# Out projection of a hybrid decoder block: the conv half of a row tile ahead of the other half, the row chain cut into stages, weights loaded as whole rows

## The chip, the cores and the metric

One core of one Trainium2 chip. The metric is the time of one execution on the device in microseconds; the kernel before took 1990.24 us, the median of three runs from 1987.65 to 1991.64.

## The reference

A decoder block on `x` of shape (1, 2048, 1024), all in float32:

```python
hn = rms_norm(x, g_pre_mix)
proj = hn @ w_in                       # 1024 -> 512 (ssm) + 3 x 512 (conv)
y_ssm  = s5_group_mixer(u_ssm, ...)    # state-space scan, gelu, y * sigmoid(y @ w_glu)
y_conv = short_conv_mixer(h, b, c, conv_w)
y = concat([rms_norm(y_ssm, g_ssm_out), rms_norm(y_conv, g_conv_out)])
x = x + rms_norm(y @ w_out, g_post_mix)
hn = rms_norm(x, g_pre_mlp)
m = square(relu(hn @ w_up)) @ w_down
x = x + rms_norm(m, g_post_mlp)
```

`w_out` is 1024 x 1024: its rows 0 to 511 take the ssm half of `y`, rows 512 to 1023 the conv half.

## The kernel before

Every float32 product is made of three matmuls (`mm3`, L88 to L90): each operand is split into a high part (an ACT copy, L169) and a low part (a subtraction on DVE or POOL, L170). A product of 128 x 512 x 128 thus costs three TensorE instructions.

The sequence is written out in four parts. First the ssm input projection; then the conv projections (three per column tile and block of 512 positions, eight passes `n` of two blocks), with the state-space work hooked between them; then the **out projection**, which the change touches; then the MLP, whose two products are computed in seven partial products each (`ORDER`, `DORDER`). The orders of TensorE and of POOL (GpSimd) are as written; DVE (VectorE), ACT (ScalarE) and SP (the DMA queue) get their order from the planner, which places work by its estimate of readiness, with the program's order as priority, and runs it in order on the chip.

The out projection goes over four blocks of 512 positions, each of four row tiles `t` of 128 rows:

- `yprep(blk)` loads the state-space output of a block and splits it.
- `cprep(blk)` loads the conv output `yc_d` of a block (four tiles of 128 x 512), multiplies by `gcv`, splits into `b8` tiles, squares and sums (`sumsq`).
- `glu(blk)` multiplies by `w_glu` (48 matmuls into PSUM tag B), then sigmoid, product, gain `gss`, split, and on POOL squares (L794) and sums (L798).
- `norms(blk, br)` sums the squares over partitions by four small matmuls (L858, PSUM tag C) and takes the -1/2 power on POOL (L868). The result `rr` scales the rows of branch `br` (1 conv, 0 ssm).
- `branch(blk, t, br, ...)` multiplies a row tile by its half of `w_out` in two column halves `dh` of twelve matmuls each. Both branches take PSUM tag A (4 banks). The conv half leaves by ACT (L890), the ssm half is added by DVE (L892). `norms` is called after the first twelve matmuls of tile 0 in each branch.
- `rows_out(blk, t, o, xx)` is the row chain: sum of squares on ACT (L897), times gain (L898), `rstd` on POOL (L122, L123), residual (L900), write `x1_d`, sum of squares (L903), gain (L904), `rstd`, scale (L906), write `hn_d`.
- `load_wo` splits `w_out` in 16 steps of 128 x 512, each staged through an `s2k` tile; 8 steps for the conv half run inside `glu(0)`, 8 for the ssm half beside the conv branches of block 0.

Between the products, `next(aside)` takes one step of side work: `yprep` and `cprep` of the next block; in block 2 also `hsums`, which writes sums of quarters of the normed rows to `hs_d` (L946, L947); in block 3 `first()`, which prepares the MLP's first operands (`wprep`, `xbuild` with transposes L984). Buffers: `s2k` 9 tiles of 2 KB per partition, `b8` 14 and `c8` 4 tiles of 8 KB, `r4("o")` and `r4("xx")` 2 tiles of 4 KB each. In blocks 1 to 3 a row tile is done as

```python
branch(blk, t, 1, o, aside)
branch(blk, t, 0, o, aside)
rows_out(blk, t, o, xx)
```

while block 0 does all four conv branches first (into `os_`, two `c8` tiles).

Of the kernel before, what the change touches and what calls it, by code (L numbers as in the profile page):

```python
# [52 lines left out]
def block_kernel(  # L53
# [641 lines left out]
    def yprep(blk):  # L695
# [7 lines left out]
        for q in range(4):  # L703
# [34 lines left out]
    for n in range(8):  # L738
        hf, i = divmod(n, 4)
        for b in range(2):  # L740
            blk = 2 * hf + b
            if g == 45:
                pl.close()
                open_left()
                run(yprep(0))
                gluh, glul = c8(), c8()
                for k in range(4):
                    split2(gluh[:, k, :], glul[:, k, :], w_glu[k * P:(k + 1) * P, :], V)
            r2 = act.tile([P, BLK], F32, name="r2", bufs=2)
# [20 lines left out]
            V.tensor_tensor(yt, ps, c, op=ALU.mult)  # L770
# [15 lines left out]
    gcv = small("gcv", 4, 1)  # L786
    nc.sync.dma_start(out=gcv, in_=g_conv)


    def sumsq(blk, br, i, t):  # L790
        if br:
            A.activation(t, t, AF.Square)
        else:
            G.tensor_tensor(t, t, t, op=ALU.mult)  # L794
        if i == 0:
            sqs[blk, br] = t
        else:
            (V if br else G).tensor_tensor(sqs[blk, br], sqs[blk, br], t, op=ALU.add)  # L798

    def cprep(blk):  # L800
        h, l = b8(), b8()
        mc[blk] = (h, l)
        raw = {}
        for i in range(-2, 4):
            if i < 2:
                raw[i + 2] = s2k()
                nc.sync.dma_start(out=raw[i + 2], in_=yc_d[i + 2][:, blk * BLK:(blk + 1) * BLK])
                if i < 0:
                    continue
            if i == 0:  # L810
                yield
            yc = raw[i]
            A.activation(h[:, i, :], yc, AF.Copy, scale=gcv[:, i:i + 1])
            V.scalar_tensor_tensor(l[:, i, :], yc, gcv[:, i:i + 1], h[:, i, :].bitcast(F32),
                                   op0=ALU.mult, op1=ALU.subtract)
            sumsq(blk, 1, i, yc)
            yield

    def glu(blk):
        h, l = b8(), b8()  # L820
        mh[blk] = (h, l)
        for m in range(4):
# [5 lines left out]
            A.activation(sg, ps, AF.Sigmoid)  # L828
# [3 lines left out]
            A.activation(h[:, m, :], sg, AF.Copy, scale=gss[:, m:m + 1])  # L832
            V.scalar_tensor_tensor(l[:, m, :], sg, gss[:, m:m + 1], h[:, m, :].bitcast(F32),
                                   op0=ALU.mult, op1=ALU.subtract)
            sumsq(blk, 0, m, sg)
            if blk == 0:
                next(wo_steps)
                next(wo_steps)

    wo = {}  # L840

    def load_wo():
        for h in (1, 0):
            for k in range(4 * h, 4 * h + 4):
                wo[k] = b8()
            for dh in range(2):
                for k in range(4 * h, 4 * h + 4):
                    t = wo[k]
                    split2(t[:, 2 * dh, :], t[:, 2 * dh + 1, :],
                           w_out[k * P:(k + 1) * P, dh * 512:dh * 512 + 512], G if k % 2 else V)  # L850
# [22 lines left out]
    def junk():  # L873
        return sb["R"].tile([P, D], BF16, name="junk", bufs=1)

    def branch(blk, t, br, o, aside):

        m = (mc if br else mh)[blk]
        for dh in range(2):
            sl = slice(dh * 512, dh * 512 + 512)  # L880
# [7 lines left out]
            rr = rrs[blk, br]  # L888
            if br:
                A.activation(o[:, sl], ps, AF.Copy, scale=rr[:, t:t + 1])  # L890
            else:
                V.scalar_tensor_tensor(o[:, sl], ps, rr[:, t:t + 1], o[:, sl], op0=ALU.mult, op1=ALU.add)  # L892
            next(aside, None)

    def rows_out(blk, t, o, xx):
        s1 = small("s1", 4)
        A.activation(junk(), o, AF.Square, accum_out=s1[:, 0:1])  # L897
        V.tensor_tensor(o, o, gpo, op=ALU.mult)  # L898
        rstd(s1[:, 1:2], s1[:, 0:1], 1, 1.0 / D, s1[:, 2:3])
# [4 lines left out]
        V.tensor_tensor(o, xx, gmb, op=ALU.mult)  # L904
        rstd(s3[:, 1:2], s3[:, 0:1], 1, 1.0 / D, s3[:, 2:3])
# [4 lines left out]
    def wout(blk, aside, between=iter(())):  # L910
        def row_in(t):
            xx = r4("xx")
            tt = 4 * blk + t
            nc.sync.dma_start(out=xx, in_=x[tt * P:(tt + 1) * P, :])
            return xx

        if blk == 0:
            os_ = [z.rearrange("p (a b) c -> p a (b c)", b=2)[:, i, :] for z in (c8(F32), c8(F32)) for i in range(2)]
            for t in range(4):
                branch(blk, t, 1, os_[t], between)  # L920
            run(between)
        for t in range(4):
            xx = row_in(t)
            o = os_[t] if blk == 0 else r4("o")
            if blk:
                branch(blk, t, 1, o, aside)
            branch(blk, t, 0, o, aside)
            if t == 3:
                run(aside)
            rows_out(blk, t, o, xx)  # L930

# [54 lines left out]
            V.tensor_tensor(l[:, k, :], pt, h[:, k, :].bitcast(F32), op=ALU.subtract)  # L986
            yield

    cprep0 = cprep(0)
    next(cprep0)  # L990
    gss = sb["XR"].tile([P, 24], F32, name="gss", bufs=1)[:, :4]
    nc.sync.dma_start(out=gss, in_=g_ssm)
    run(cprep0)
# [27 lines left out]
    def first():  # L1021
# [334 lines left out]
```

## Time and profile before

| | |
|---|---|
| median of three runs | 1990.24 us (1987.65 to 1991.64) |
| the profiled execution | 1990.73 us, span 1988.8 us, mean granted clock 0.983 |
| TensorE busy (matmul) | 1920.9 us, 97% |
| VectorE, ScalarE, GpSimd busy | 71%, 44%, 37% |
| instructions | 25438 |

The span runs from the first to the last instruction of the profiled execution. Busy time is the share of the span in which an engine executes; on TensorE matmuls overlap, so a busy engine can still run slowly. Rows in order of time give start, duration, engine, line, operation and `out<-in` by the program's names, and in brackets how long the engine was idle before it and what released it. Rows of waits give who waited for whom, the total in us, the times and the longest. Rows of stretches give the length, then busy time and count of PE, PEld, DVE, ACT and POOL, the granted clock, the DMA share and GB/s.

### The profile page before, as it was taken

The page shows a single profiled execution, that of the slowest core. Times are in us where ns is not written, and L with a number is a line of the kernel's source. Part 1 is how long each engine was busy: PE and PEld are TensorE (multiplying, and loading weights), DVE is VectorE, ACT ScalarE, POOL GpSimd, SP SyncE. Part 2 cuts the span into 40 slices and gives each one's busy share as a digit, 9 for nine tenths or more (in the row PEclk, how much of TensorE's full clock was granted, in tenths as well). Part 3 has the DMA queues.
Part 4 walks back from the last instruction along what each step waited for, and adds up shares of the span by engine and source line. Part 5 has one row for each costly group of instructions (what it writes and reads, how often), then busy time and mean ns, then how long its engine had stood idle before and what let it go on. Part 6 is the DMA issues. An engine that isn't in the chain of part 4 may idle for free.

```text
span 1988.8 us, 25438 instructions
## 1 busy us (share of the span) xinstructions
PE 1920.9 (97%) x8576; PEld 1572.0 (79%) x8576; DVE 1402.3 (71%) x2007; ACT 865.4 (44%) x1479; POOL 741.4 (37%) x727
## 2 busy tenths in 40 slices
PE   8899999998899799999999999999999999999996
PEld 6677777776787678888888888887888888888885
DVE  8958889856666668998888878877644344539554
ACT  6322232226454355555566555554334242335321
POOL 3666556304534533434433434433522002104222
PEclk9899999998999899999999999999999999999998
DMA  6432343235546566555446434428955545538633
GB/s 203 133 101 75 99 123 115 70 90 160 179 157 194 189 243 218 211 204 204 170 166 238 158 143 148 148 86 312 382 168 180 187 147 180 195 107 301 236 114 111
DMA packets 202002, 340.34 MB, mean 171 GB/s; under 512 B 56336, under 2 KB 64784, under 8 KB 199568
## 3 DMA queue, kind: packets, MB, share of 16 engines
q1 hardware_dynamic: 200576, 336.62, 50.2%
q10 hardware_dynamic: 1296, 2.10, 0.3%
q8 instruction: 67, 1.10, 0.2%
q14 instruction: 63, 0.52, 0.1%
HBM read 230.51 MB, written 106.95 MB: 170 GB/s over the span
## 4 chain that ended last, share of the span: by engine, by line
PE 80%; POOL 6%; DMA 4%; DVE 4%; issue 3%; ACT 2%; SPq 0%; DVEq 0%; POOLq 0%; ACTq 0%
PE A L89 16%; PE A L88 16%; PE A L90 16%; PE mm L88 4%; PE mm L89 4%; PE mm L90 4%; PE B L88 4%; PE B L89 4%; PE B L90 4%; PE C L89 1%; PE C L88 1%; PE C L90 1%; DMA raw<-in_xt_dram 1%; PE B L984 1%; POOL s2k L794 1%
## 5 line engine op out<-in xcount | busy, mean ns | idle before, releaser
L1016 POOL TENSOR_TENSOR t<-b 128x512 f32<-128x512 f32 x155 | 243.8, 1595 | 358.6 <-ACT w2a L169 98.3
L1130 POOL TENSOR_TENSOR t<-t,t 128x512 f32<-128x512 f32 x80 | 116.8, 1468 | 356.1 <-DMA t<-in_w_down_dram 306.5
L88 PE MATMUL mm<-xh,wh 128*128 128x512 f32 x496 | 199.3, 402 | 7.8 <-ACT wh L169 7.3
L89 PE MATMUL mm<-xl,wh 128*128 128x512 f32 x496 | 195.6, 394 | 2.1 <-DVE xl L153 2.1
L90 PE MATMUL mm<-xh,wl 128*128 128x512 f32 x496 | 195.2, 393 | 0.2 <-POOL wl L170 0.2
L170 DVE TENSOR_TENSOR b<-w2b,b 128x512 fp32r<-128x512 f32 x112 | 92.4, 864 | 134.1 <-ACT b L169 134.1
L88 PE MATMUL A<-b,c 128*128 128x512 f32 x448 | 174.5, 390 | 1.0 <-ACT b L169 1.0
L89 PE MATMUL A<-b,c 128*128 128x512 f32 x448 | 174.6, 390 | 0.6 <-DVE b L170 0.6
L90 PE MATMUL A<-b,c 128*128 128x512 f32 x448 | 174.4, 389 | 0.0
L88 PE MATMUL A<-b,w2b 128*128 128x512 f32 x384 | 150.1, 391 | 0.0
L90 PE MATMUL A<-b,w2b 128*128 128x512 f32 x384 | 149.5, 389 | 0.0
L89 PE MATMUL A<-b,w2b 128*128 128x512 f32 x384 | 149.5, 389 | 0.0
L170 DVE TENSOR_TENSOR c<-w2a,c 128x512 fp32r<-128x512 f32 x112 | 81.2, 764 | 95.8 <-ACT c L169 95.8
L1103 DVE TENSOR_TENSOR t<-t,t 128x512 f32<-128x512 f32 x160 | 126.7, 858 | 22.9 <-ACT t L1057 22.9
L169 ACT ACTIVATE b<-w2b 128x512 fp32r<-128x512 f32 x112 | 64.7, 623 | 158.4 <-PE C L90 144.7
L89 PE MATMUL B<-b,b 128*128 128x512 f32 x336 | 130.8, 389 | 0.0
L88 PE MATMUL B<-b,b 128*128 128x512 f32 x336 | 130.7, 389 | 0.0
L90 PE MATMUL B<-b,b 128*128 128x512 f32 x336 | 130.7, 389 | 0.0
L169 ACT ACTIVATE c<-w2a 128x512 fp32r<-128x512 f32 x112 | 64.9, 624 | 135.3 <-PE A L90 134.1
L88 PEld LDWEIGHTS mm<-xh,wh 128*128 128x128 f32 x496 | 94.4, 190 | 34.0 <-ACT wh L169 7.3
L88 PE MATMUL A<-b,b 128*128 128x512 f32 x256 | 107.2, 419 | 6.2 <-DVE o L892 2.3
L89 PEld LDWEIGHTS mm<-xl,wh 128*128 128x128 f32 x496 | 94.4, 190 | 21.6 <-DVE xl L153 2.9
(438 smaller groups left out, 4910.4 us busy)
## 6 DMA issues: line engine op xcount, KB each, us to landing
hid_d<-t SPq DMA_DIRECT2D x224, 256.0 KB
t<-in_w_down_dram SPq DMA_DIRECT2D x192, 256.0 KB
b<-in_w_up_dram SPq DMA_DIRECT2D x64, 512.0 KB
w2b<-hid_d SPq DMA_DIRECT2D x112, 256.0 KB
w2a<-hid_d SPq DMA_DIRECT2D x112, 256.0 KB
raw<-in_xt_dram SPq DMA_DIRECT2D x48, 256.0 KB
raw<-in_w_cv_dram SPq DMA_DIRECT2D x48, 256.0 KB
b<-hs_d SPq DMA_DIRECT2D x10, 1024.0 KB
```

The source lines that it names most:

```text
L88: T.matmul(ps, lh, rh, start=start, stop=False)
L89: T.matmul(ps, lh, rl, start=False, stop=False)
L90: T.matmul(ps, ll, rh, start=False, stop=stop)
L169: A.activation(dst_h, raw, AF.Copy)
L170: eng.tensor_tensor(dst_l, raw, dst_h.bitcast(F32), op=ALU.subtract)
L794: G.tensor_tensor(t, t, t, op=ALU.mult)
L984: T.transpose(pt[:, t * P:(t + 1) * P], r[:, t, k * P:(k + 1) * P], ident)
L1016: eng.tensor_tensor(src, q[0], q[1], op=pm_op[LEFT[j][1]])
L1103: V.tensor_tensor(src, q[0], q[1], op=pm_op[LEFT[j][1]])
L1130: G.tensor_tensor(r[0], r[0], r[1], op=pm_op[RIGHT[j][1]])
```

## The change

1. `gcv` lies in a constant tile and is loaded earlier; `cprep(0)` is run ahead of the last block of the conv projections and puts its splits in the two free `c8` tiles.
2. `load_wo` loads a row of `w_out` whole (128 x 1024, 512 KB) into `r4` tiles: four ahead for the conv half, two ahead for the ssm half. The splits stay 16, POOL for odd rows, DVE for even ones. In `glu(0)` the sums of squares are moved behind the loop, so on POOL they follow the splits.
3. `branch` takes tag A for conv and tag B (3 banks, shared with `glu`) for ssm. In blocks 1 to 3 the order is conv 0, conv 1, `norms(blk, 0)`, ssm 0, conv 2, ssm 1, conv 3, ssm 2, ssm 3. In block 0 all four conv tiles come first, then `norms(0, 0)`, then the ssm tiles; its `os_` are `b8` tiles.
4. `rows_out` is a generator of three stages; the second and third are taken by `row_step`, called after each half product and after each `m` of `glu`.
5. In `first()`, `wprep` makes its sums on POOL, not DVE.

```diff
@@ at g == 45
+                run(cprep(0))
@@ glu
+            if blk == 0:
+                sgs.append(sg)
+                next(wo_steps)
+                if m:
+                    next(wo_steps)
+            else:
+                sumsq(blk, 0, m, sg)
+            row_step()
+        for m, sg in enumerate(sgs):
             sumsq(blk, 0, m, sg)
@@ load_wo
-            for dh in range(2):
-                for k in range(4 * h, 4 * h + 4):
-                    split2(..., w_out[k * P:(k + 1) * P, dh * 512:dh * 512 + 512], G if k % 2 else V)
+            for at in range(-4 if h else -2, 4):
+                ahead = at + (4 if h else 2)
+                if ahead < 4:
+                    raw[ahead] = r4("xx" if h and ahead > 1 else "o")
+                    nc.sync.dma_start(out=raw[ahead], in_=w_out[k * P:(k + 1) * P, :])
+                ...
+                for dh in range(2):
+                    split(..., raw[at][:, dh * 512:dh * 512 + 512], G if at % 2 else V)
                     yield
@@ branch
-            ps = pst("A")
+            ps = pst("A" if br else "B")
...
-            if t == 0 and dh == 0:
-                norms(blk, br)
+            if t == 0 and dh == 0 and br:
+                norms(blk, 1)
+            yield pss
             next(aside, None)
+            row_step()
+    def row_step():
+        for g in list(rowq):
+            if next(g, 0) == 0:
+                rowq.remove(g)
+    def ssm_rows(blk, t, o, xx, aside):
+        for dh, pss in enumerate(branch(blk, t, 0, aside)):
+            ssm_out(blk, t, o, pss[dh], dh)
+            if dh:
+                g = rows_out(blk, t, o, xx)
+                next(g)
+                rowq.append(g)
+    def wout(blk, aside):
+        for t in range(5):
+            if t < 4:
+                for cps[t] in branch(blk, t, 1, aside):
+                    pass
+            if t == 1:
+                norms(blk, 0)
+            if t:
+                xx, o = row_in(blk, t - 1), r4("o")
+                conv_out(blk, t - 1, o, cps.pop(t - 1))
+                ssm_rows(blk, t - 1, o, xx, aside)
+        run(aside)
@@ first
-                wprep(0, n, V, s2k)
+                wprep(0, n, G, s2k)
```

More of the change, by code (lines that the diff above doesn't have):

```diff
@@ L620, in block_kernel @@
     next(params)
-    cw = const.tile([P, LINE], F32, name="cw")[:, :12].rearrange("p (a b) -> p a b", b=4)
+    cwt = const.tile([P, LINE], F32, name="cw")
+    gcv = cwt[:, 12:16]
+    nc.sync.dma_start(out=gcv, in_=g_conv)
+    cw = cwt[:, :12].rearrange("p (a b) -> p a b", b=4)
     nc.sync.dma_start(out=cw, in_=conv_w)
@@ L708, in yprep, with sumsq, cprep @@
             yield
+    def sumsq(blk, br, i, t):
+        if br:
+            A.activation(t, t, AF.Square)
+        else:
+            G.tensor_tensor(t, t, t, op=ALU.mult)
+        if i == 0:
+            sqs[blk, br] = t
+        else:
+            (V if br else G).tensor_tensor(sqs[blk, br], sqs[blk, br], t, op=ALU.add)
+    def cprep(blk):
+        h, l = (b8(), b8()) if blk else (c8(), c8())
+        mc[blk] = (h, l)
+        raw = {}
+        for i in range(-2, 4):
+            if i < 2:
+                raw[i + 2] = s2k()
+                nc.sync.dma_start(out=raw[i + 2], in_=yc_d[i + 2][:, blk * BLK:(blk + 1) * BLK])
+                if i < 0:
+                    continue
+            if i == 0:
+                yield
+            yc = raw[i]
+            A.activation(h[:, i, :], yc, AF.Copy, scale=gcv[:, i:i + 1])
+            V.scalar_tensor_tensor(l[:, i, :], yc, gcv[:, i:i + 1], h[:, i, :].bitcast(F32),
+                                   op0=ALU.mult, op1=ALU.subtract)
+            sumsq(blk, 1, i, yc)
+            yield
     events = {}
@@ L784, in pst @@
         return psB.tile(list(shape), F32, name=tag, bufs={"A": 4, "B": 3, "C": 1}[tag])
[L786 to L817, printed above, removed]
     def glu(blk):
@@ L834, in glu @@
                                    op0=ALU.mult, op1=ALU.subtract)
+            if blk == 0:
[3 more added lines that the diff above has]
+                    next(wo_steps)
+            else:
+                sumsq(blk, 0, m, sg)
+            row_step()
+        for m, sg in enumerate(sgs):
             sumsq(blk, 0, m, sg)
-            if blk == 0:
-                next(wo_steps)
-                next(wo_steps)
     wo = {}
@@ L845, in load_wo @@
                 wo[k] = b8()
[L846 to L850 removed]
+            raw = {}
+            for at in range(-4 if h else -2, 4):
+                ahead = at + (4 if h else 2)
+                if ahead < 4:
+                    raw[ahead] = r4("xx" if h and ahead > 1 else "o")
+                    k = 4 * h + ahead
+                    nc.sync.dma_start(out=raw[ahead], in_=w_out[k * P:(k + 1) * P, :])
+                if at < 0:
+                    continue
+                t = wo[4 * h + at]
+                for dh in range(2):
+                    split(t[:, 2 * dh, :], t[:, 2 * dh + 1, :], raw[at][:, dh * 512:dh * 512 + 512],
+                          G if at % 2 else V)
                     yield
@@ L885, in branch, with conv_out, ssm_out @@
                     (w[:, 2 * dh, :], w[:, 2 * dh + 1, :]), k == 0, k == 3)
-            if t == 0 and dh == 0:
-                norms(blk, br)
[L888 to L892, printed above, removed]
-            next(aside, None)
+            if t == 0 and dh == 0 and br:
+                norms(blk, 1)
+            yield pss
+            next(aside, None)
+            row_step()
+    def conv_out(blk, t, o, pss):
+        for dh, ps in enumerate(pss):
+            A.activation(o[:, dh * 512:dh * 512 + 512], ps, AF.Copy, scale=rrs[blk, 1][:, t:t + 1])
+    def ssm_out(blk, t, o, ps, dh):
+        sl = slice(dh * 512, dh * 512 + 512)
+        V.scalar_tensor_tensor(o[:, sl], ps, rrs[blk, 0][:, t:t + 1], o[:, sl], op0=ALU.mult, op1=ALU.add)
     def rows_out(blk, t, o, xx):
@@ L908, in rows_out, with row_in, wout_first @@
         nc.sync.dma_start(out=dst, in_=o.rearrange("p (k c) -> p k c", k=2))
[L910 to L921, printed above, removed]
-        for t in range(4):
[L923 to L930, printed above, removed]
+    def row_in(blk, t, name="xx"):
+        xx, tt = r4(name), 4 * blk + t
+        nc.sync.dma_start(out=xx, in_=x[tt * P:(tt + 1) * P, :])
+        return xx
+    def ssm_rows(blk, t, o, xx, aside):
[5 more added lines that the diff above has]
+                rowq.append(g)
+    def wout_first(aside):
+        os_ = [z.rearrange("p (a b) c -> p a (b c)", b=2)[:, i, :] for z in (b8(F32), b8(F32)) for i in range(2)]
+        for t in range(4):
+            for pss in branch(0, t, 1, aside):
+                pass
+            conv_out(0, t, os_[t], pss)
+        run(aside)
+        norms(0, 0)
+        for t in range(4):
+            ssm_rows(0, t, os_[t], row_in(0, t, "xx" if t < 2 else "o"), aside)
+    def wout(blk, aside):
+        cps = {}
+        for t in range(5):
+            if t < 4:
+                for cps[t] in branch(blk, t, 1, aside):
+                    pass
+            if t == 1:
[4 more added lines that the diff above has]
+                ssm_rows(blk, t - 1, o, xx, aside)
+        run(aside)
     ORDER = (1, 4, 5, 7, 3, 2, 6)
@@ L987, in xbuild @@
             yield
-    cprep0 = cprep(0)
-    next(cprep0)
+    wo_steps = load_wo()
+    next(wo_steps)
     gss = sb["XR"].tile([P, 24], F32, name="gss", bufs=1)[:, :4]
     nc.sync.dma_start(out=gss, in_=g_ssm)
-    run(cprep0)
     gpo = sb["R"].tile([P, D], F32, name="gp", bufs=1)
@@ L1035, in both @@
             yield
-    wout(0, iter(()), both(wo_steps, chain(yprep(1), cprep(1))))
+    wout_first(both(wo_steps, chain(yprep(1), cprep(1))))
     glu(1)
@@ L1043, in block_kernel @@
     wout(3, first())
+    while rowq:
+        row_step()
     pm_.close()
```

11 lines of the change are left out of this document (7 added, 4 removed).

## The prediction

> **What bounds the kernel now.** I read the page first, then PE's waits, PE's rows in order of time, the busy time by stage, and last what POOL, DVE and the DMA queue do in the out projection.
>
> ```profile
> span 1988.8 us, 25438 instructions
> PE 1920.9 (97%) x8576; PEld 1572.0 (79%) x8576; DVE 1402.3 (71%) x2007; ACT 865.4 (44%) x1479; POOL 741.4 (37%) x727
> ```
>
> TensorE is busy 97% of the span, so only what keeps it idle or slow is worth anything. The waits of PE between 430 and 770 us, the stretch of the out projection (line, what it waited for: us in total, times, longest):
>
> ```profile
> PE C L858 <- POOL s2k L798: 10.9, 3, 6.2
> PE B L88 <- ACT s2k L828: 4.1, 1, 4.1
> PE A L89 <- POOL b L170: 3.0, 4, 1.4
> PE A L89 <- DVE b L170: 2.9, 3, 1.3
> PE A L88 <- DVE o L892: 2.3, 2, 1.7
> PE A L88 <- ACT b L169: 2.0, 1, 2.0
> PE A L88 <- ACT b L832: 1.8, 1, 1.8
> PE A L90 <- DVE b L833: 0.5, 1, 0.5
> ```
>
> These are 27.5 us: 7.9 for weight splits (L169, L170), 10.9 for POOL's sums of squares of the ssm half (L798 feeds `norms`), 8.7 for the rest. PE's rows (start, duration) mark the borders of the four row blocks, each beginning with `glu`:
>
> ```profile
> 446.07 0.47 PE L88 MATMUL B<-w2a,c 128*128 128x512 f32 x1 [0.88 <-DVE wrk L770]
> 457.07 0.39 PE L88 MATMUL A<-b,b 128*128 128x512 f32 x1
> 517.96 0.39 PE L88 MATMUL B<-w2a,c 128*128 128x512 f32 x1
> 528.84 0.39 PE L88 MATMUL A<-b,b 128*128 128x512 f32 x1
> 531.56 0.95 PE L858 MATMUL C<-ones,s2k 128*128 128x1 f32 x8
> 532.37 0.49 PE L88 MATMUL A<-b,b 128*128 128x512 f32 x1
> 583.45 0.39 PE L88 MATMUL B<-w2a,c 128*128 128x512 f32 x1
> 647.90 0.39 PE L88 MATMUL B<-w2a,c 128*128 128x512 f32 x1
> 687.81 0.60 PE L984 MATMUL C<-ident,b 128*128 128x128 f32 x4
> 688.16 0.48 PE L88 MATMUL A<-b,b 128*128 128x512 f32 x1
> 724.31 0.39 PE L88 MATMUL A<-c,w2a 128*128 128x512 f32 x1
> ```
>
> Undisturbed, `glu` takes 528.84 - 517.96 = 10.88 us, twelve matmuls of a half product 531.56 - 528.84 = 2.72, one `norms` 0.81. A block is 10.88 + 16 x 2.72 + 2 x 0.81 = 56.0; the last also has 8 transpose groups of 0.35, so 58.8. Measured: 71.9, 65.5, 64.5 and 76.4. The losses are **15.9, 9.5, 8.4 and 17.6, together 51.4 us**. Waits explain 27.5 of that. The other 24 are slow clock, seen in the busy times by stretch (PE, PEld, DVE, ACT, POOL, then the granted clock, DMA share and GB/s):
>
> ```profile
> 457.10:476.50 19.40, 12.23 (x34) 7.66 (x33) 12.88 (x13) 7.51 (x13) 16.18 (x12) 0.72 0.65 164
> 605.30 1.56 PE L858 MATMUL C<-ones,s2k 128*128 128x1 f32 x8 [1.70 <-POOL s2k L798]
> 606.00:607.00 1.00, 1.00 (x6) 1.00 (x6) 0.74 (x2) 0.49 (x1) 0.22 (x1) 0.50 0.00 0
> 612.00:613.00 1.00, 1.00 (x5) 0.81 (x4) 0.57 (x1) 0.00 (x0) 1.00 (x2) 0.75 0.00 0
> ```
>
> In the stretch with the weight waits the mean clock was 0.72. After the single wait of 1.70 us that ended at 605.30 it was 0.50, though PE was busy again, and in the microsecond from 612 still 0.75: near 6.9 us at half speed, 3.4 us lost. So a wait costs itself plus some 3.4.
>
> **The change, part by part.** Block 0 first. `cprep(0)` moves ahead of the last 72 projection matmuls and takes `c8` tiles. It issues four loads of 256 KB, whose place on SP is little changed (SP carries no other wait that PE feels there), and 4 ACT copies, 4 ACT squares, 4 DVE splits, 3 DVE adds.
>
> ```profile
> L814 DVE SCALAR_TENSOR_TENSOR b<-s2k,gcv,b x16: 743/748/753, 450.8 to 643.0; 128x512 fp32r<-128x512 f32 x16
> L813 ACT ACTIVATE b<-s2k,gcv x16: 687/714/725, 449.7 to 641.5; 128x512 fp32r<-128x512 f32 x16
> 430.00:445.20 15.20, 15.20 (x68) 12.24 (x66) 9.80 (x12) 7.37 (x9) 0.51 (x1) 1.00 0.80 216
> ```
>
> With a square and an add taken like these rows, DVE gets 7 x 0.75 = 5.2 us and has 15.2 - 9.8 = 5.4 idle there: just covered, and the last DVE product of that stage (L770, on which the first `glu` matmul waits 0.88) can slip. I charge 1 us (0 to 2). The early load of `gcv` on SP, ahead of `cw`, delays SP by one issue far from any wait: nothing.
>
> The weights of the conv half were split half row by half row, staged through `s2k`, and their loads stood in the queue until buffers came free; on POOL the splits alternated with the sums.
>
> ```profile
> 456.76 10.46 SPq L686 DMA_DIRECT2D s2k<-in_w_out_dram  x7
> 458.09 1.78 POOL L170 TENSOR_TENSOR b<-s2k,b 128x512 fp32r<-128x512 f32 x1 [0.51 <-ACT b L169]
> 475.50 1.02 POOL L868 TENSOR_TENSOR rr<-sr,nhalf 128x4 f32<-128x4 f32 x1
> 445.20:457.10 11.90, 11.03 (x49) 9.12 (x49) 7.86 (x11) 7.41 (x13) 1.24 (x1) 1.00 0.75 249
> L794 POOL TENSOR_TENSOR s2k<-s2k 128x512 f32<-128x512 f32 x16 | 23.3, 1458 | 19.4 <-DVE b L833 18.1 <-DMA s2k<-in_w_out_dram 0.6 <-DVE sr L864 0.6
> L798 POOL TENSOR_TENSOR s2k<-s2k 128x512 f32<-128x512 f32 x12 | 18.8, 1564 | 0.9
> ```
>
> Now four rows of 512 KB go into `r4` tiles, which lie where the projection's tiles were, so they are issued from about 446.5, after the first `glu` matmul (446.07). At the 249 GB/s of that stretch 2.1 MB need 8.4 us, so the last lands near 456. POOL splits its two halves in 1.5 to 1.8 each: 459.5 to 460. PE needs the first of them at 457.07 + 10 x 0.227 = 459.3: the weight waits are nearly gone. But POOL now does its seven sums behind the splits, 4 x 1.46 + 3 x 1.56 = 10.5 us, then the `pow` (1.02) that all conv outputs need. `conv_out(0)` thus ends near 472.4. PE is through two conv tiles at 457.07 + 4 x 2.72 + 0.81 = 468.8 and then has no free A bank of the four: **a new wait of 3.6 us, plus 3.4 of slow clock**. Block 0 keeps a loss of 7.0, a gain of 8.9. Bounds: 15.9 (POOL at its shortest) and -3 (rows landing 6 us late with POOL always at 1.78, so that `rr` comes 10 us later than I put it). The four later loads (ssm half) reuse the `o` tiles two deep and are due only at the first ssm tile, 16 us on: nothing.
>
> At this place a rule can be weighed. By the rows at 605 to 613 a wait of 1.7 us already brings the half clock. The Trainium skill, "TensorE: Matmul & The Clock Gate", section "HAM oscillation — how this bites in real kernels", has it return only for idle gaps over about 3.4 us; the trace differs, and with its rule the new wait would hardly cost more than itself, yet the gaps that go would return no clock either.
>
> Blocks 1 and 2: two conv tiles now precede `norms(blk, 0)` in place of a conv tile and half an ssm tile, so the ssm sums are due 10.88 + 4 x 2.72 + 0.81 = 22.6 us after the block begins, not 19.85. The last add of the sums in the three blocks:
>
> ```profile
> 542.19 1.26 POOL L798 TENSOR_TENSOR s2k<-s2k 128x512 f32<-128x512 f32 x1
> 603.98 1.26 POOL L798 TENSOR_TENSOR s2k<-s2k 128x512 f32<-128x512 f32 x1
> 679.68 1.26 POOL L798 TENSOR_TENSOR s2k<-s2k 128x512 f32<-128x512 f32 x1
> 654.66 1.29 POOL L946 TENSOR_TENSOR s2k<-c 128x512 f32<-128x512 f32 x1 [1.97 <-DVE o L892]
> 653.77 1.40 DVE L892 SCALAR_TENSOR_TENSOR o<-A,rr,o 128x512 f32<-128x512 f32 x2
> ```
>
> They ended 25.5, 21.8 and 33.0 us into their blocks. In block 2 that is early enough already: its wait of 1.70 and the half clock go, 8.4 - 2.3 = **6.1**. In block 1 the last row's second `rstd` (L122, L123) now stands behind the first sum instead of ahead of it, and ACT's scaling with it; about 3 us earlier would do, I take a remaining loss of 1.5, so **8.0** (3.1 if only the order on PE helps: 2.9 wait and 3.5 clock stay). What is late next is the `pow` for conv, at 23 us, due when the third conv tile wants an A bank at 29: covered.
>
> End of block 2 and block 3 (17.6 plus the 2.3 of L892): POOL's rstd of rows 2 and 3 queue behind the `hsum` operations, which wait for writes of `hs_d` and ran until 656, 8 us into block 3. Their places in the list of side steps are the same after the change. The later due time gives 2.72, the reordered `rstd` some 3: I take **6**; bounds 0 (the write chain sets the time) and 17. The ssm products moving to the three B banks that `glu` and `xbuild` use is free while L892 follows within 5.4 us; at that border it came 5.9 after PE's end. `wprep` on POOL: three sums more there, 5 us by the 1.6 of a POOL operation, three off DVE; nothing unless they hold `rr` by more than the B banks cover.
>
> After the projection: with conv ahead, rows 2 and 3 end close together, so one row chain more reaches the start of the MLP, where DVE is already full:
>
> ```profile
> 740.00:756.00 16.00, 11.80 (x62) 10.26 (x61) 15.50 (x25) 12.18 (x23) 0.64 (x1) 0.89 0.43 160
> ```
>
> I charge 2 us (0 to 5). Sum: 8.9 + 8.0 + 6.1 + 6 - 1 - 2 = **26.0 us**. The profiled execution took 1990.73 us (span 1988.8 and 1.9 around it), 0.5 above the median 1990.24 of three; 1964.7 by the one, **1964 us** by the other.
>
> **Rivals.** (a) POOL takes the weights' place: block 0 gives nothing, because `rr` waits for splits and sums in one queue. For it: POOL was busy 16.2 of 19.4 us there; against it: two splits are then shorter than before. 1973 us. (b) The chain of `hs_d` writes holds: the 6 go, and half of block 2's 6.1 is swallowed. For it: DVE and POOL both waited on those writes; 1973. With (a) and (b), 1982. (c) All stalls go, the row chain in stages frees POOL early: 8.9 + 5 more in block 0, 11 more in block 3, 1.5 more in block 1, 43.5 in all: 1947. (d) The other side: `glu` needs a B bank that `ssm_out` of the last row holds. PE comes to it 5.44 us after that product. If DVE, blocked in order by the row chain, is 10 us late, 5.3 + 3.4 are lost at each of four borders (the last is `xbuild`), 35 us against 26: 1999. It decides from about 8.5 us late; the latest border of the trace, block 3's, shows 5.9. (e) The short waits do not cause the half clock: then 4.3 + 4.3 + 1.7 + 3.5 - 3 = 11 us, 1979. The Trainium skill's page named above would have it so; the rows at 605 to 613 speak against it.
>
> **How the numbers follow.** Forecast (1955 to 1970) 0.5, (a) or (b) alone 0.16, both 0.05, (c) 0.12, (d) 0.08, (e) 0.03, the change without effect 0.06. A measurement of this kernel tells some 0.2%, 4 us, from no change. Faster by more: 0.5 + 0.16 + 0.05 + 0.12 + 0.03 = 0.86, from which I take 0.02 for the low end of both; within: 0.06; slower 0.08 and those 0.02. The range 1946 to 1984 takes in (c), (a), (b), both and (e).
>
> **What would show it.** Right: no L169/L170 waits of PE after 457; a single wait on A near 469 released by ACT; blocks of about 63, 57.5, 58; no PE wait on POOL's sums in blocks 1 and 2; clock 1.00 there; the row chains' `rstd` between the sums. Wrong: PE waiting on B in `glu` for DVE's `ssm_out`; weight rows landing after 460; the `hs_d` writes still ending 8 us into the last block; a longer DVE backlog after it.

## The result, and the profile after

The changed kernel took **2002.31 us**, the median of five runs (1998.82 to 2003.36), against 1990.24 (1986.16 to 1994.23) for the kernel before in as many. The ratio is 1.0059, 95% interval 1.004 to 1.0078: slower by 0.6%, where 1.3% faster was forecast. The profiled execution took 2003.36 us with a span of 2001.6, 12.8 above the span before. Its page:

```profile
span 2001.6 us, 25417 instructions
PE 1922.0 (96%) x8576; PEld 1575.3 (79%) x8576; DVE 1400.0 (70%) x2004; ACT 862.7 (43%) x1479; POOL 736.1 (37%) x730
```

TensorE does the same work in 12.8 us more: it waits or runs slowly somewhere. The stretches of the four row blocks, cut as in the prediction at the first `glu` matmul of each and at the first MLP matmul, say where (bounds, length, PE busy and count, granted clock, DMA share, GB/s). First the kernel before, then after:

```profile
446.07:517.96 71.89, 63.92 (x256) 0.91 0.49 150
517.96:583.45 65.49, 60.65 (x258) 0.92 0.60 189
583.45:647.90 64.45, 60.42 (x258) 0.95 0.62 187
647.90:724.31 76.41, 65.66 (x289) 0.91 0.54 190
```

```profile
448.31:514.70 66.39, 61.70 (x256) 0.92 0.55 179
514.70:577.28 62.58, 59.17 (x257) 0.95 0.44 138
577.28:655.27 77.99, 63.77 (x257) 0.87 0.65 205
655.27:736.04 80.77, 67.13 (x289) 0.87 0.51 177
```

Start +2.2, block 0 -5.5, block 1 -2.9, **block 2 +13.5, block 3 +4.4**, rest +1.1 (2001.6 - 736.04 = 1265.6 against 1264.5): together +12.8. The change gained 8.4 us in the first two blocks and lost 17.9 in the other two. The three largest waits of PE from 440 to 745 us (total, times, longest), and their places in time in the rows of PE (in the changed kernel `ssm_out` is L922, `conv_out` L918, `norms` L875, the sums L721, the sigmoid L830, the row chain's squares L926 and L933, `hsum` L995, `xbuild` L1033 to L1035):

```profile
PE B L88 <- DVE o L922: 10.1, 2, 6.9
PE C L875 <- DVE c L1035: 7.7, 1, 7.7
PE C L875 <- POOL s2k L721: 7.5, 2, 4.1
```

```profile
448.31 0.47 PE L88 MATMUL B<-w2a,c 128*128 128x512 f32 x1 [1.55 <-DVE wrk L803]
540.98 1.23 PE L875 MATMUL C<-ones,s2k 128*128 128x1 f32 x5 [3.40 <-POOL s2k L721]
583.41 0.50 PE L88 MATMUL B<-w2a,c 128*128 128x512 f32 x1 [3.24 <-DVE o L922]
609.41 1.87 PE L875 MATMUL C<-ones,s2k 128*128 128x1 f32 x8 [4.08 <-POOL s2k L721]
649.99 0.80 PE L88 MATMUL B<-b,b 128*128 128x512 f32 x1 [6.90 <-DVE o L922]
681.32 0.63 PE L1033 MATMUL C<-ident,b 128*128 128x128 f32 x4 [2.87 <-DMA b<-hs_d]
689.70 1.83 PE L875 MATMUL C<-ones,s2k 128*128 128x1 f32 x8 [7.75 <-DVE c L1035]
```

The sums of the ssm half are still waited for (3.40 and 4.08). New are 3.24 + 6.90 us on a B bank that a late `ssm_out` holds, and in block 3 a `norms` that waits 7.75 us for the only C bank, which `xbuild` took 8.4 us earlier.

**Block 2, read by its rows.** The square at the head of each row's chain, on ACT, is the clock of the row chain. First the kernel before, rows 0 to 2 of block 2; then the changed kernel, rows 0 to 3 of block 1 and 0 to 2 of block 2:

```profile
616.60 1.06 ACT L897 ACTIVATE junk<-o 128x1024 bf16<-128x1024 f32 x1 [5.92 <-DVE o L892]
630.56 1.04 ACT L897 ACTIVATE junk<-o 128x1024 bf16<-128x1024 f32 x1
645.02 1.06 ACT L897 ACTIVATE junk<-o 128x1024 bf16<-128x1024 f32 x1 [0.64 <-DVE o L892]
```

```profile
555.46 1.06 ACT L926 ACTIVATE junk<-o 128x1024 bf16<-128x1024 f32 x1 [1.42 <-DVE o L922]
567.79 1.06 ACT L926 ACTIVATE junk<-o 128x1024 bf16<-128x1024 f32 x1
580.28 1.05 ACT L926 ACTIVATE junk<-o 128x1024 bf16<-128x1024 f32 x1
587.91 1.04 ACT L926 ACTIVATE junk<-o 128x1024 bf16<-128x1024 f32 x1
...
624.08 1.06 ACT L926 ACTIVATE junk<-o 128x1024 bf16<-128x1024 f32 x1
639.91 1.06 ACT L926 ACTIVATE junk<-o 128x1024 bf16<-128x1024 f32 x1 [0.74 <-DVE o L922]
652.23 1.06 ACT L926 ACTIVATE junk<-o 128x1024 bf16<-128x1024 f32 x1 [1.37 <-DVE o L922]
```

PE needs 10.9 us for the products of a row; the chain of block 2 ran at some 14 us a row in both kernels (28.4 us from the first to the third square before, 28.2 after). So from the first square on the rows set the pace in this block, not PE. Block 2 ended 2.9 us after the third row's square before and 3.0 after, and the third square came 13.4 us later into the block (75.0 against 61.6). That is the block's loss. All of it is there at the first square, 46.8 us into the block against 33.2. The matmul of `norms(2, 0)`, which needs the sums, came 32.1 us into the block against 21.9 (605.30 - 583.45): 10.3 of the 13.6. The rest, 3.4, was lost between the sums and the square. What made the sums late should be `glu(2)`, whose elementwise work stands behind the rows of block 1; rows 0 to 2 of it came 12.4 us apart (the run e7 below tests this). Their order on ACT, and how POOL and DVE passed lateness on in block 2 (rows of three engines):

```profile
579.13 1.26 ACT L918 ACTIVATE o<-A,rr 128x512 f32<-128x512 f32 x2 [3.61 <-DMA hn_d<-o]
```

```profile
629.75 1.87 POOL L995 TENSOR_TENSOR s2k<-c 128x512 f32<-128x512 f32 x1 [7.68 <-DMA hs_d<-s2k]
631.71 0.19 POOL L122 TENSOR_SCALAR s<-s 128x1 f32<-128x1 f32 x1
643.32 1.26 POOL L995 TENSOR_TENSOR s2k<-c 128x512 f32<-128x512 f32 x1 [5.44 <-DVE s2k L721]
644.66 0.19 POOL L122 TENSOR_SCALAR s<-s 128x1 f32<-128x1 f32 x1
```

```profile
645.52 1.28 DVE L930 SCALAR_TENSOR_TENSOR xx<-o,s,xx 128x1024 f32<-128x1024 f32 x1 [2.28 <-POOL s L123]
649.19 0.74 DVE L922 SCALAR_TENSOR_TENSOR o<-B,rr,o 128x512 f32<-128x512 f32 x1
```

At 579.13 the conv scaling of block 1's last row waits 3.61 us for the write of `hn_d` that frees one of the two `o` tiles, and the square of the row ahead of it (580.28) stands behind it on ACT. In block 2 the `rstd` of a row (631.71, 644.66) stands on POOL behind an `hsum` that waits 7.68 and 5.44 us for a buffer; DVE's residual (645.52) waits for that `rstd`, the next `ssm_out` (649.19) stands behind it, with a gain and two of DVE's `hsum` operations between them, and PE gets its B bank at 649.99.

### The profile page after: what moved, and what is told of

It is laid out like the page before. It is cut to its first block, busy times and chain, and to the rows that moved or that the text cites. A ratio compares the mean times of both kernels' runs of the same rounds, so it can differ in the third digit from the quotient of the medians.

```text
span 2001.6 us, 25417 instructions
## 1 busy us (share of the span) xinstructions
PE 1922.0 (96%) x8576; PEld 1575.3 (79%) x8576; DVE 1400.0 (70%) x2004; ACT 862.7 (43%) x1479; POOL 736.1 (37%) x730
## 4 chain that ended last, share of the span: by engine, by line
PE 75%; POOL 7%; DVE 6%; DMA 4%; ACT 3%; issue 3%; SPq 1%; DVEq 0%; POOLq 0%; ACTq 0%
PE A L88 15%; PE A L89 15%; PE A L90 15%; PE B L88 4%; PE B L89 4%; PE B L90 4%; PE mm L88 4%; PE mm L89 4%; PE mm L90 4%; DMA raw<-in_xt_dram 2%; PE C L89 1%; PE C L90 1%; PE C L88 1%; POOL s L122 1%; DVE xx L930 1%
## 5 line engine op out<-in xcount | busy, mean ns | idle before, releaser
L88 PE MATMUL B<-b,b 128*128 128x512 f32 x464 | 186.1, 401 | 9.9 <-DVE o L922 6.9
L89 PE MATMUL A<-b,c 128*128 128x512 f32 x480 | 188.7, 393 | 3.1 <-DVE b L170 1.8
L88 PE MATMUL A<-b,c 128*128 128x512 f32 x480 | 188.4, 393 | 3.2 <-ACT b L169 2.9
L90 PE MATMUL A<-b,c 128*128 128x512 f32 x480 | 188.1, 392 | 0.0
L89 PE MATMUL B<-b,b 128*128 128x512 f32 x464 | 185.0, 399 | 0.0
L90 PE MATMUL B<-b,b 128*128 128x512 f32 x464 | 184.6, 398 | 0.0
L169 ACT ACTIVATE b<-w2b 128x512 fp32r<-128x512 f32 x112 | 64.7, 622 | 158.8 <-PE C L90 145.2
L88 PEld LDWEIGHTS B<-b,b 128*128 128x128 f32 x464 | 90.0, 194 | 29.3 <-DVE o L922 7.3
```

The lines of the kernel that those rows point to most:

```text
L88: T.matmul(ps, lh, rh, start=start, stop=False)
L89: T.matmul(ps, lh, rl, start=False, stop=False)
L90: T.matmul(ps, ll, rh, start=False, stop=stop)
L169: A.activation(dst_h, raw, AF.Copy)
```

## The experiments

Each run was timed beside the kernel before on the same chip; ratios are to it. Block lengths are from one profiled execution each, which in some runs (e12, e17 and e18 among them) was the slowest of all. What follows block 3 is not in the table: it took 1264.5 us in the kernel before, 1265.6 in the changed one and from 1264.4 to 1270.3 in the others, so blocks alone do not add up to a time.

| run | median us | ratio (95% interval) | blocks 0 to 3, us |
|---|---|---|---|
| before | 1990.24 | | 71.9, 65.5, 64.5, 76.4 |
| the change | 2002.31 | 1.0059 (1.0040 to 1.0078) | 66.4, 62.6, 78.0, 80.8 |
| e1, no conv-ahead | 1993.38 | 1.0015 (1.0005 to 1.0024) | 66.6, 65.8, 66.3, 78.4 |
| e2, no stages | 1999.30 | 1.0041 (1.0029 to 1.0053) | 66.4, 62.4, 80.1, 74.5 |
| e3, neither | 1984.29 | 0.9973 (0.9964 to 0.9981) | 66.4, 65.4, 63.9, 73.9 |
| e4, late `xbuild` | 1991.12 | 1.0009 (1.0000 to 1.0018) | 66.4, 61.7, 78.5, 68.1 |
| e5, ssm on A | 2001.05 | 1.0058 (1.0045 to 1.0070) | 66.5, 67.4, 73.0, 74.5 |
| e6, no `hsum` | 1991.23 | 1.0010 (1.0001 to 1.0019) | 66.5, 62.7, 65.3, 78.8 |
| e7, own `o` rows | 1992.76 | 1.0015 (1.0006 to 1.0024) | 66.4, 62.8, 66.9, 80.4 |
| e8, old order in block 2 | 1990.79 | 1.0004 (0.9995 to 1.0012) | 66.6, 62.8, 72.3, 73.0 |
| e9, e4 + e7 | 1981.38 | 0.9960 (0.9948 to 0.9972) | 66.4, 62.4, 68.2, 69.7 |
| e10, e9 + squares on ACT | 1968.88 | 0.9899 (0.9886 to 0.9912) | 66.4, 56.8, 64.7, 65.4 |
| e11, e9 + `hsum` on DVE | 1974.14 | 0.9926 (0.9914 to 0.9938) | 66.5, 61.1, 64.4, 66.6 |
| e12, e9 without stages | 1981.07 | 0.9962 (0.9950 to 0.9975) | 66.6, 62.5, 68.4, 68.9 |
| e13, change + squares | 1993.24 | 1.0023 (1.0013 to 1.0033) | 66.4, 59.0, 75.1, 76.8 |
| e14, before + squares | 1982.87 | 0.9968 (0.9956 to 0.9979) | 69.8, 62.7, 63.1, 73.2 |
| e15, change + `hsum` on DVE | 1995.97 | 1.0032 (1.0020 to 1.0045) | 66.5, 62.7, 76.6, 74.4 |
| e16, all four | 1966.57 | 0.9887 (0.9874 to 0.9901) | 66.4, 56.6, 62.2, 63.8 |
| e17, e3 + squares + `hsum` | 1970.62 | 0.9904 (0.9889 to 0.9919) | 66.4, 62.2, 58.8, 69.5 |
| e18, e16 without stages | 1969.96 | 0.9894 (0.9877 to 0.9910) | 66.5, 56.5, 62.8, 67.5 |

### Which part costs: a two by two

e1 puts the old order back in blocks 1 to 3, with both products on A and `norms(blk, 0)` behind the first ssm half (the main part of the edit):

```diff
-        for t in range(5):
...
-                conv_out(blk, t - 1, o, cps.pop(t - 1))
-                ssm_rows(blk, t - 1, o, xx, aside)
+        for t in range(4):
+            xx, o = row_in(blk, t), r4("o")
+            for dh, pss in enumerate(branch(blk, t, 1, aside)):
+                A.activation(o[:, dh * 512:dh * 512 + 512], pss[dh], AF.Copy, scale=rrs[blk, 1][:, t:t + 1])
+            ssm_rows(blk, t, o, xx, aside)
```

> The changed kernel with the old order in blocks 1 to 3: per row tile the conv product, its scaling, then the ssm product, both on the A banks, norms(blk, 0) after the first ssm half; the row chain in stages, the whole weight rows, the early cprep(0) and wprep on POOL stay. Theory T1, conv-ahead (ssm products on the B banks that glu and xbuild use, conv scaling ahead of the row before's square on ACT): blocks 2 and 3 fall back to about 66 and 77 us, PE no longer waits on a B bank in glu for ssm_out, time about 1984 us (1978 to 1988). Theory T2, the staged row chain delays rows and sums: little changes, 1998 to 2004. Theory T3, only the order on the one C bank in block 3: blocks 1 and 2 stay at 63 and 78, block 3 too; 2000 to 2004.

e2 keeps conv-ahead and issues each row chain whole:

```diff
-                g = rows_out(blk, t, o, xx)
-                next(g)
-                rowq.append(g)
+                run(rows_out(blk, t, o, xx))
```

> The changed kernel with each row chain issued whole behind its last ssm_out, as before; conv-ahead stays. T1: the B bank waits and the 12 us row period stay, 1998 to 2006 us. T2: rows end earlier, sums of squares of the ssm half are done by 24 us into each block, block 2 about 66 us, time 1982 to 1990. T3: block 3 keeps about 80 us and its wait on norms(3,0), block 2 unchanged, 1999 to 2005.

e3 has both edits.

> Both undone together: only the whole weight rows, the early cprep(0), the order of sums in block 0 and wprep on POOL are left of the change. If block 0's gain of 5.5 us and the start's charge of 2.2 are the weights' own, and blocks 1 to 3 go back to 65.5, 64.5 and 76.4: 1990 - 5.5 + 2.2 = 1987 us (1983 to 1990). If the weight part itself pushes work into the later blocks (T4), 1990 to 1998. Together with the two before it makes a two by two of conv-ahead and staging: T1 has it equal to the run without conv-ahead, T2 equal to the run without stages.

With stages, taking conv-ahead out gives 0.44% (1.0059 to 1.0015, intervals apart) and block 2 is back at 66.3: T1 has the place right, and T3, by which block 2 would not have moved, falls for that block. e1 was 9 us above T1's figure, because stages cost too: with the old order 0.42% (1.0015 to 0.9973, apart). With conv-ahead the intervals overlap (e2), and block 2 stays at 80 where T2 had 66: taking the stages out of the change as made is not shown to help. What is left of the change in e3, whole weight rows with the early `cprep(0)`, the sums of block 0 behind the splits and `wprep` on POOL, is together **faster than before**, 0.9973; T4 falls. None of these four was run alone. Counted from e3, conv-ahead alone (e2) costs 0.68%, stages alone (e1) 0.42%, both 0.86%. So the loss comes from conv-ahead first and from stages second, not from the weights.

### Block 3: one C bank

e4 puts one side step ahead of the first `xbuild`:

```diff
+            if i == 0:
+                yield
             yield from xbuild(0, j)
```

> The changed kernel with one more step ahead of the first xbuild in the last block, so that its transposes (one C bank) come after norms(3,0) on PE. T3: the 7.7 us wait of norms(3,0), the 2.9 us wait of the transpose on the hs_d reload and the half clock behind them go, block 3 shrinks from 80.8 to about 68 us, time 1988 to 1992. T1 and T2: the wait is taken up by the sums of squares (they ended at 682.6, norms(3,0) could go at about 683 in place of 689.7), 3 to 6 us less: 1996 to 2000.

Block 3 fell from 80.8 to 68.1, the time to 1991. The rows of PE in e4:

```profile
680.95 1.30 PE L875 MATMUL C<-ones,s2k 128*128 128x1 f32 x8 [4.04 <-POOL s2k L721]
686.39 0.66 PE L1033 MATMUL C<-ident,b 128*128 128x128 f32 x4
```

`norms(3, 0)` now goes ahead of the transposes and waits 4.04 for the sums in place of 7.75 for the bank. T3 is right for its block and only for it: block 2 stays at 78.5. In the changed kernel the bank was held because ACT's copy out of it (L1034) stood behind the conv scalings of four column halves, which waited for `rr`. The first of them and the copy, rows of ACT in the changed kernel:

```profile
684.89 0.69 ACT L918 ACTIVATE o<-A,rr 128x512 f32<-128x512 f32 x1 [6.75 <-DVE rr L887]
...
688.22 0.61 ACT L1034 ACTIVATE c<-C 128x512 fp32r<-128x512 f32 x1
```

### Block 2: bank, buffers or hsum

e5 moves the ssm products of blocks 1 to 3 to A:

```diff
-            ps = pst("A" if br else "B")
+            ps = pst("A" if br or blk else "B")
```

> The changed kernel with the ssm products of blocks 1 to 3 on the A banks, conv-ahead and stages kept. Theory T1b, sharing the three B banks is what costs: the waits on B in glu (3.2 and 6.9 us, with 3.4 of half clock each) go and only a part returns as a wait on A two products later; block 2 about 68 us, 1986 to 1992. Theory T5, the rows themselves are late (ssm_out done 3 to 9 us after the border because DVE and ACT stand behind the row chain), so that whatever waits next takes the wait up: ACT's sigmoids, glu's elementwise work, then the sums: block 2 76 to 79 us, 1999 to 2004.

The time did not change (2001). Rows of PE in e5:

```profile
566.57 0.50 PE L88 MATMUL A<-b,b 128*128 128x512 f32 x1 [2.47 <-ACT o L918]
636.20 0.80 PE L88 MATMUL A<-b,b 128*128 128x512 f32 x1 [6.05 <-DVE o L922]
```

The wait moved to the A banks. The shared B bank is where the lateness shows, not where it comes from; T1b falls. T5 gave the time, and its figure for block 2 (76 to 79) was missed: 73.0. Block 3 was shorter too (74.5); block 1 (67.4) and what follows block 3 (1270.1 against 1265.6) were longer.

e6 leaves out the half sums:

```diff
+            if hf == 0:
+                nc.sync.dma_start(out=hs_d[hf][j][:, t, :], in_=u[:, 2 * k0 + b0, :])
+                continue
```

> The changed kernel with the 20 half sums of the first half left out (hs_d is written straight from the tile that they read; the DMAs stay): no hsum work on POOL and DVE, no s2k buffers for it in block 2. T5 with hsum as the holder (POOL's rstd of rows 0 and 1 stand 5.5 and 3.5 us behind hsum operations that wait for s2k buffers): the row chain of block 2 runs at 11 us a row, the wait of 6.9 us at its end goes, block 2 about 67 us; block 3 gains 3 more by earlier reloads; 1984 to 1990. T6, the two o buffers (conv scaling of row t+2 waits for row t's write, ahead of row t+1's square on ACT) set the period whatever POOL does: block 2 75 to 78 us, 1996 to 2001.

e7 gives block 1 four `o` rows:

```diff
+        os_ = [z.rearrange("p (a b) c -> p a (b c)", b=2)[:, i, :] for z in (c8(F32), c8(F32)) for i in range(2)] if blk == 1 else None
...
-                xx, o = row_in(blk, t - 1), r4("o")
+                xx, o = row_in(blk, t - 1), os_[t - 1] if os_ else r4("o")
```

> The changed kernel with four rows of their own for o in block 1 (two c8 tiles that lie free there), so that no conv scaling in block 1 waits for the write of the row two before. T6: block 1's row period falls from 12.4 to about 11 us, its last ssm_out comes at 582 in place of 586, the 3.24 us wait in glu(2) shrinks below 1 and the sums of block 2 end 3 us earlier; time 4 to 8 us less than the changed kernel, 1994 to 1998. T5 without o: row period stays at 12 us, 2000 to 2004.

Either of them brings block 2 down, to 65.3 and 66.9. T5 and T6 both expected the other's repair to fail: neither is the whole cause. The squares in block 1 of e7:

```profile
556.00 1.06 ACT L926 ACTIVATE junk<-c 128x1024 bf16<-128x1024 f32 x1 [1.42 <-DVE c L922]
563.66 1.04 ACT L926 ACTIVATE junk<-c 128x1024 bf16<-128x1024 f32 x1
574.22 1.06 ACT L926 ACTIVATE junk<-c 128x1024 bf16<-128x1024 f32 x1 [2.83 <-DVE c L922]
581.85 1.04 ACT L926 ACTIVATE junk<-c 128x1024 bf16<-128x1024 f32 x1
```

From the first to the fourth 25.9 us, where the changed kernel took 32.5. Its gain, larger than T6 had it, comes in block 2 and not in block 1. A table of the squares (us into block 2) shows how the two work:

| | first square | third square | block ends |
|---|---|---|---|
| before | 33.2 | 61.6 | 64.5 |
| the change | 46.8 | 75.0 | 78.0 |
| e7, own `o` rows | 37.7 | 66.4 | 66.9 |
| e6, no `hsum` | 41.5 | 65.8 | 65.3 |
| e13, change + squares | 43.6 | 72.1 | 75.1 |
| e10 | 34.7 | 63.7 | 64.7 |
| e16, all four edits (below) | 34.9 | 60.0 | 62.2 |
| e17, old order with squares and `hsum` (below) | 31.1 | 55.4 | 58.8 |

e7 has `norms(2, 0)` 24.8 us into the block in place of 32.1, starts the rows of block 2 9.1 us sooner and leaves their pace (28.7); e6 starts them 5.3 sooner and quickens the pace to 24.3. The block ends from 0.5 us before to 3.3 us after the third square.

e8 has the old order in block 2 alone, with e4's edit (the main part of the edit):

```diff
+        if blk == 2:
+            for t in range(4):
...
+                ssm_rows(blk, t, o, xx, aside)
+            run(aside)
+            return
```

> The changed kernel with the old order of conv and ssm in block 2 alone (there the hsum work lies) and the late xbuild of the last block. By the blocks of the runs so far: 66.4, 62 (ahead), 65 (old order), 68 to 70 (ahead, late xbuild), rest 1266.7 and start 447.5: 1976 to 1982 us, faster than the kernel before. If the gains of the blocks do not add (late rows only handed on to the next block): 1984 to 1988.

A miss of both ranges, by 9 and by 3 us: block 2 fell to 72.3 only, for its `glu` still had the late rows of block 1 to wait for (PE waits 2.48 on `ssm_out`, 4.04 on the sums). The late rows are handed on.

e9 has e4 and e7 together.

> The changed kernel with the two repairs together: rows of their own for o in block 1, and the late xbuild in block 3. Alone they took about 10 and 11 us off. Theory A, two separate losses (block 2 by late rows, block 3 by the one C bank): they add, blocks 66.4, 62.8, 66.9, 68 and 1266.7 after a start of 448: 1979 to 1983 us, faster than the kernel before. Theory B, one loss that moves (a late row chain found somewhere): at most 4 us below the better of the two, 1987 to 1992.

Theory A holds: 1981.4, 0.4% faster than the kernel before.

### The sums, hsum and the stages

e10, on top of e9:

```diff
-        if br:
+        if br or blk:
             A.activation(t, t, AF.Square)
```

> As the run with both repairs, and the four squares of the ssm half in blocks 1 to 3 on ACT in place of POOL (3 x 4 operations, 1.0 to 1.9 us each on POOL). If POOL's own work makes the sums late (they are waited for 3 to 4 us in each of the blocks 1 to 3): the waits on the sums fall by 2 to 3 us each and their half clock goes in some, 6 to 15 us less than with both repairs alone. If the sums are late because ACT and DVE hold glu's elementwise products behind the row chain of the block before: within 3 us of it, or slower because ACT gets four more operations.

e11, on top of e9:

```diff
-                hsum(0, t - 1, us[t - 1], s2k, (1, 6))
+                hsum(0, t - 1, us[t - 1], s2k, ())
```

> As the run with both repairs, and the eight hsum operations of block 2 that POOL does moved to DVE, so that no rstd of a row stands behind a hsum that waits for a buffer. If POOL's order is the whole of it, block 2 falls by the 5 us wait on ssm_out and its half clock, 5 to 8 us less. If the s2k buffers are, DVE now stands before them and holds ssm_out itself: 0 to 8 us more.

e12 is e9 with e2's edit.

> As the run with both repairs, with each row chain issued whole, conv-ahead kept. If stages cost time by themselves (9 us more with the old order, 3 with conv-ahead): 3 to 6 us less than with both repairs. If with conv-ahead and rows in time they pay as meant: 2 to 8 us more, with block 2 at 70 or above.

e10 takes 12.5 us off e9, and block 1 stands at 56.8 where 56.0 was reckoned as undisturbed. The stretch of block 1 in e10:

```profile
513.54:570.36 56.82, 56.55 (x258) 1.00 0.46 144
```

So POOL's own operations were what kept the sums late. e11 gains 7 us by taking eight `hsum` operations off POOL; whether their length counted or their place ahead of the `rstd` was not told apart. e12 is not told apart from e9: with the rows in time the stages cost and bring nothing that these runs can tell.

### Do they need each other

e13 is the changed kernel with e10's edit alone, e14 the kernel before with it, e15 the changed kernel with e11's alone, e16 all four edits.

> The changed kernel as it is, with only the squares of the ssm half in blocks 1 to 3 on ACT. If late sums start the loss: block 1 57 us, block 2 about 66 us, while block 3 keeps its C bank wait (norms(3,0) behind xbuild), 80: 1975 to 1984. If the o buffers and hsum make it alone: block 1 57, block 2 still 75 to 78, block 3 80: 1992 to 1997.

> The kernel before, with only the squares of the ssm half in blocks 1 to 3 on ACT. Its waits on POOL's sums were 10.9 us in three places, with about as much of half clock. If ACT takes them without delaying the sigmoids: 1990 less 12 to 18: 1972 to 1978, and then the gain of the squares is not the change's. If the old order's tight place is ACT's sigmoid chain (waits of 1.8 and 4.1 us on it): 0 to 6 us less, 1984 to 1990.

> The changed kernel as it is, with only the eight hsum operations of POOL moved to DVE. If rstd behind hsum is what makes block 2 long: block 2 65 to 68 us, block 3 about 78: 1989 to 1993. If the late rows of block 1 (o buffers) are needed too: block 2 72 to 76, 1995 to 2000.

> Both repairs, the squares on ACT and hsum on DVE. If the rest adds: 66.4, 56.8, 61 to 62, 62 to 63 and 1265 after 447: 1961 to 1964 us. If DVE becomes the bound in block 2 (it takes hsum as well as the row chain): 1966 to 1970.

e13 and e15 leave block 2 at 75.1 and 76.6: neither the squares nor the place of `hsum` takes the loss away without e7's rows, as the second theory had it each time. e6 had brought block 2 to 65.3 without these rows, but it leaves out all 20 sums and their buffers; which of that counts beyond POOL's eight is open. e14: the squares give the old order 6.6 us, between the two ranges that were put and about half of what they give e9; this much of the gain is not the change's. e16 was 3 to 6 us above the figure for adding up, within that of the second theory, and its interval is not apart from e10's.

> The old order and the whole row chains (as in the run with both undone: whole weight rows and early cprep left), with the squares of the ssm half on ACT and hsum on DVE. If conv-ahead pays only once the sums are in time: about 6 to 8 us less than with both undone, 1975 to 1980, against 1966.6 with conv-ahead and its repairs. If the repairs of squares and hsum are all there is to gain: 1964 to 1969.

> All four repairs with conv-ahead, each row chain issued whole. If stages still cost nothing or a little: 1962 to 1968. If they pay now that rows run in time: 1969 to 1976, with the loss in blocks 2 and 3 and at the start of the MLP.

e17 is e3 with the squares and `hsum` edits, e18 is e16 with e2's. Both theories for e17 missed, the first (1975 to 1980) by 4 us, the second (1964 to 1969) by 2: the old order gains 13.7 us from the two edits, nearly as much as the change with its repairs (14.8, e9 to e16). Between e16, e17 and e18 the intervals overlap. By the medians conv-ahead with its repairs is worth 4 us over the old order, and that is not shown. In the profiles of e16 and e17 conv-ahead, with its repairs and the stages, gains 5.6 in block 1 and 5.7 in block 3 and loses 3.4 in block 2. That loss is there at the first square of the block (34.9 us into it against 31.1). e18 came out at the low end of the second theory, with its loss in block 3 (67.5 against 63.8).

## Why the prediction was wrong, point by point

The sum said -26.0 us. By its terms, gains as positive:

| term | predicted | measured | what the runs showed |
|---|---|---|---|
| `cprep(0)` ahead | -1 | -2.2 | L803 is waited for 1.55 in place of 0.88; in the other runs with the same code up to there the border lay from 446.7 to 450.1 |
| block 0, weights | +8.9 | +5.5 | weight waits 4.3 us in place of 7.9, the wait on A only 0.36 |
| block 1, sums | +8.0 | +2.9 | the sums ended 26.2 us into the block, no earlier than before (25.5) |
| block 2 | +6.1 | -13.5 | the failed step |
| border and block 3 | +6 | -4.4 | the C bank, not among the rivals |
| MLP start | -2 | -1.1 | about as charged |

**The step that failed** is "free while L892 follows within 5.4 us". It weighed conv-ahead only against PE's own need of a bank, and the 6.1 for block 2 took it that the sums would still end 21.8 us into the block; `norms(2, 0)` had to wait for them until 32.1. The rows of the kernel before, quoted above, already showed a chain that took 14 us for a row of block 2 where PE takes 10.9. On such a chain what counts is when the first row starts and how fast the rows go. Conv-ahead starts the first row later, by 3.8 us even with the sums in time (e16 against e17) and by 13.6 in the change as made, and it makes `conv_out` ask for its `o` tile earlier on ACT, ahead of the square of the row before. The prediction followed every tile that the weights and the squares use, and never counted `o`, two tiles deep.

Rival (d) had the sign, the waiting instruction (PE on B in `glu`, for `ssm_out`), and with 1999 nearly the time; it was given 0.08. Its mechanism was half right: e5 shows that another bank changes nothing, and of its four borders one showed the wait (583.41), while the larger came inside block 2 (649.99).

**The sums.** The 8.0 for block 1 rested on "about 3 us earlier would do"; 3.1 stood beside it ("if only the order on PE helps"), and 2.9 came. The last `rstd` of block 0 did go behind the first square, as put (528.27), but the sums ended no earlier. In these rows of POOL in block 1 the first square waits for `glu`'s product and stands 11.7 us into the block, and the second waits for the next product; the last row is the last add:

```profile
526.43 1.77 POOL L717 TENSOR_TENSOR s2k<-s2k 128x512 f32<-128x512 f32 x1 [4.21 <-DVE b L835]
528.27 0.78 POOL L122 TENSOR_SCALAR s<-s 128x1 f32<-128x1 f32 x1
532.34 1.48 POOL L717 TENSOR_TENSOR s2k<-s2k 128x512 f32<-128x512 f32 x1 [2.66 <-DVE b L835]
539.66 1.26 POOL L721 TENSOR_TENSOR s2k<-s2k 128x512 f32<-128x512 f32 x1
```

The place of that `rstd` hardly matters: in e2, where the row chains are whole and it stands ahead of the first square, the sums ended 25.4 us into the block, and block 1 was as long (62.4). What helps is less work on POOL: with the squares on ACT `norms(1, 0)` goes some 23 us into the block (e10 and e13) in place of 26.3.

**Block 0.** The 8.9 missed the order of ACT. (The loads of the weight rows were also issued from 448.56, 2.1 us later than put.) ACT, in the planned order, had sigmoid and gain of `glu(0)` ahead of the copies of the second row, which follow with no idle time; then POOL took 3.4 us for each row's two halves, as put. Rows of ACT, then of POOL:

```profile
460.01 1.32 ACT L834 ACTIVATE b<-s2k,gss 128x512 fp32r<-128x512 f32 x2
461.23 1.14 ACT L169 ACTIVATE b<-o 128x512 fp32r<-128x512 f32 x2
```

```profile
461.93 3.40 POOL L170 TENSOR_TENSOR b<-o,b 128x512 fp32r<-128x512 f32 x2 [19.23 <-ACT b L169]
478.92 1.03 POOL L885 TENSOR_TENSOR rr<-sr,nhalf 128x4 f32<-128x4 f32 x1
```

The `pow` ended at 479.95, so `conv_out(0)` could not end by the 472.4 that was put, and rival (a)'s mechanism was there. PE hardly felt it (0.36 us on A), because the weights had kept PE itself back.

**Block 3.** The prediction asked when the `hs_d` writes end and when `rr` comes. It did not ask which of two users of the single C bank is issued first. e4, one step moved, is worth 12.7 us there.

**What was right.** The waits on the sums and the half clock behind them are the reserve: e10 frees block 1 of both, and the clock of that block is 1.00. e16 ends at 1966.6, near the 1964 that was forecast. But it takes four further edits, two of which bring the old order to 1970.6 as well.

## What to carry to other kernels

Before moving matmuls ahead, compare the pace of the chain behind them with TensorE's, row by row in the profile: where the chain was slower, in block 2 here, TensorE's order bought nothing, and what delayed the chain's first row lengthened the block by as much (13.6 and 13.5 us). For each resource that the moved step takes (two `o` tiles, one C bank), ask in which order its users are issued after the move and what the in-order engine that serves it holds back. When a wait moves from one bank to another without changing the time, as in e5, look for who is late and not for who is in the way.

## What the runs showed of the hardware

A short wait of TensorE does not always bring the half clock, as the prediction's 3.4 us for each had it. Rows and stretches of PE: first the run e3, then e6, each a wait and the ten microseconds around it (length, busy, granted clock, DMA share, GB/s):

```profile
601.85 0.49 PE L875 MATMUL C<-ones,s2k 128*128 128x1 f32 x3 [1.72 <-POOL s2k L721]
...
600.00:610.00 10.00, 8.28 (x41) 1.00 0.01 2
```

```profile
584.67 0.50 PE L88 MATMUL B<-w2a,c 128*128 128x512 f32 x1 [2.45 <-DVE o L922]
...
582.00:592.00 10.00, 7.55 (x33) 1.00 0.93 335
```

After 1.72 and 2.45 us the clock stays at 1.00; in the kernel before 1.70 us brought it to 0.50. In the changed kernel 3.24 and 3.40 us did too (the clock was 0.50 from 585 to 587 and from 541 to 546). The Trainium skill, "TensorE: Matmul & The Clock Gate", section "What's actually happening", has activity judged in free-running windows of about 3.4 us; then it would matter where a wait falls in a window, which is compatible with these rows. Its rule that only idle gaps over about 3.4 us count, in "HAM oscillation — how this bites in real kernels", is not borne out by the 1.70 and the 3.24; the 3.40 lies on its edge. The new wait of 3.6 us that the prediction put in block 0 is over that bound too, so "hardly cost more than itself" did not follow from the rule. No run placed a wait on purpose, so the reason is not shown.
